# Per-call entries for the weight stream's fill table in the three mixers, and three weight low parts per layer on VectorE

## The chip, the cores and the metric

The kernel runs on one core of one Trainium2 chip. The metric is the device time of one execution, in microseconds. One program computes one inference step of a two-layer network and is written in Bass with the Tile framework: the framework puts every instruction into the queue of its engine, in an order that its scheduler decides at build time, and adds the semaphores.

## The reference, cut to what matters

T = 640 tokens (128 of a prompt, 512 latent) of width D = 1024 pass through two layers. All is float32.

```
h = h + gate_a * MixerBlock(RMSNorm(h) * (1 + scale_a) + shift_a)
h = h + gate_f * SwiGLU(RMSNorm(h) * (1 + scale_f) + shift_f)
MixerBlock: one input projection feeds three branches
  A  multi-head latent attention (8 heads, softmax per block of 128 queries)
  B  bidirectional gated linear attention (GLA; 4 heads, chunks of 64, a state from chunk to chunk)
  C  bidirectional gated DeltaNet (short convolution on q/k/v, decay per head, chunks of 64, a state)
  each branch -> 1024 by its own projection, merged by per-channel sigmoid gates, one output projection
```

## The kernel before, in words

**Products.** Activations lie with channels on the 128 partitions and tokens along the row, as tiles of 128x640. A product with a weight is made of three products of rounded parts: high weight by high activation, high by low, low by high (`mm_k`, L469 to L475). Each is two matmuls of 128x320, so one 128-row step of the contraction is six matmuls on L474. `gm` is their PSUM tile, `xh`/`xl` the parts of the layer's input, `oh`/`ol` those of a branch's output, `ah`/`al` those of the feed-forward.

**The stream.** Nearly all weight products of a layer stand in one list of fixed order, class `Stream` (L284), object `G`: the input projection column by column, then the gates, the branch projections and so on. One *piece* is one such step of six matmuls (`step`), entered in the books at 0.82 us. Weights come for four steps at a time: `wload` (L452) puts a DMA of 256 KB in the queue of SP, and `wsplit` (L460) makes the high part `wh` on ACT (L465, a Copy that rounds) and the low part `wl` on POOL (L466, a subtraction); three such splits may be alive. When the last step of a product has been issued, its `post` runs, which takes the result out of PSUM.

**The fill sites.** The mixers (DeltaNet, attention, GLA, and the state chains, "ch", which belong to the DeltaNet) have chains of small operations across PE, ACT, DVE and POOL. Between these the code calls `fill(name)` (L1502), which looks up a number of microseconds in the table `FILL` (L217) under "site@layer" and lets `G` emit pieces until that debt is paid, as long as the next product's post is registered. A site inside a loop has one number for all its calls. At a few places `G.to(name)` forces everything up to a named product and clears the debt. So the table decides how many pieces of a fixed list stand in which gap, and what an early site takes is missing later: at `G.to` before the merge of the branches the list always stands at the same place. The Tile scheduler then moves instructions by priorities of its own (a split is put ahead by 50), so a piece stands near its site, not at it.

**Sites and lines that matter here.** `l2b`, `prekk`, `vtok`, `kk_products1` belong to the DeltaNet's preparation; `advance1`, `advance2`, `queries1` to attention (L1052 ff.: scores `psc` L1141/L1147, exponential and scaling `pp` on ACT L1152/L1154, turning `ppt` L1162, values `pmo` L1179); `s01` to `s44` to GLA (`gla`, L1258 ff.: chunk products `gpa` L1343, `pu` L1370, then the state chain on DVE, L1378, a run of 14 dependent operations that writes `S`, then the output `gpo` L1395 and L1398, its norm on ACT and DVE L1400 to L1407, and the turn `gpt` L1417); `steps` to the DeltaNet's state chain (matmuls `ch` L922, DVE L947, L959, L973, ACT L962). The four GLA heads are interleaved by head; the attention's blocks are advanced by a scheduler of calls of which the last have no other stage beside them. `decays` (L786) prepares the DeltaNet's decay factors with two 128x640 tiles per pair of heads: DVE L792, POOL L793, ACT L794, POOL L796; its products with the keys are `pk`, L804.

Of the kernel before, what the change touches and what calls it, by code (L numbers as in the profile page):

```python
# [13 lines left out]
ALU = mybir.AluOpType  # L14
AX = mybir.AxisListType
PSUM = bass.MemoryType.PSUM
DRAM = bass.MemoryType.DRAM
# [121 lines left out]
def _layout(inp):  # L139
# [130 lines left out]
}  # L270
OPT = {
    'lat': 'dk0', 'dec': 1, 'l2': 1, 'tick': 3, 'gla0': 1, 'ng2': 7, 'st': 10, 'mc': 20, 'msite': [3], 'ng0':
# [11 lines left out]
class Stream:  # L284
    """Matrix products in a fixed order, emitted piece by piece between other work."""

# [86 lines left out]
def tile_hybrid(ctx: ExitStack, tc, a):  # L373
    nc = tc.nc
    ve, se, ge, pe = nc.vector, nc.scalar, nc.gpsimd, nc.tensor
# [71 lines left out]
    def prio(name):  # L447
# [4 lines left out]
        tc.cur_priority = p + tc.cur_priority - q  # L452

    def wload(src):
        with prio("pl"):
            wr = wp.tile([P, 512], F32, name="wr", tag="wr")
            dma(wr[:, :src.shape[-1]], src)
            return wr

    def wsplit(wr, kt):  # L460
        w = kt * P
        with prio("pw"):
            wh = wp.tile([P, 512], F32R, name="wh", tag="wh")
            wl = wp.tile([P, 512], F32R, name="wl", tag="wl")
            se.activation(wh[:, :w], wr[:, :w], AF.Copy)  # L465
            ge.tensor_tensor(wl[:, :w], wr[:, :w], wh[:, :w], op=ALU.subtract)  # L466
            return wh, wl
# [32 lines left out]

    # ---- modulation
    def mod_load(f, pool_):
# [19 lines left out]
    class ModVe:  # L522
        """Products of the condition with rows of the modulation weights, in single steps of the vector engine."""

# [57 lines left out]

    # ---- residual, norms
    HS = (slice(0, HF), slice(HF, T))
# [70 lines left out]
    def join(name, hs, nm, after, pre=None):  # L655
        """The last residual tile, the norm and its use, by halves of the tokens."""
        if pre:
# [9 lines left out]

    # ---- DRAM scratch
    NB = [dp.tile([4, 2, NCH, 64, 64], F32, name=f"NB{d}") for d in range(2)]
# [6 lines left out]

    # ---- gated DeltaNet
    def gdn_gates(prm, misc, gp, X, fill):
# [108 lines left out]
    def decays(p, E, SC, SCn, gp):  # L787
        N_ = []
        for d in range(2):
# [3 lines left out]
            ge.tensor_tensor(x, x, cst("negf" if d == 0 else "negb").unsqueeze(1).to_broadcast([P, NCH, 64]), op=ALU.add)  # L793
            se.activation(x, x, AF.Exp)  # L794
            N_.append(gp.tile([P, NCH, 64], F32, name="nn", tag="nn", bufs=4))
            ge.tensor_tensor(N_[d], x, SCn[:, :, i].unsqueeze(2).to_broadcast([P, NCH, 64]), op=ALU.mult)  # L796
# [23 lines left out]
    def turn_pairs(src, dst, scale):  # L820
        """Both heads of a pair from channels to tokens, chunk by chunk."""
        pv = psg("pvt").rearrange("p a (j c) -> p (a j) c", c=P)
# [12 lines left out]
    def gdn_solve(lp):  # L835
        Bb = lp.tile([P, 10, P], F32, name="Bb")
        ge.memset(Bb, 0.0)
        for d in range(2):
# [26 lines left out]
            for f in range(2):  # L865
# [11 lines left out]
                def narrow(w):  # L877
                    """Bb[:, g].T @ w[:, g] for all g, by the narrow operand and a turn."""
                    pw = psb([P, 3, P], "pw")
# [148 lines left out]

    # ---- latent attention
    def latents(l, prm, misc, M, pj, gg, fill):  # L1030
# [223 lines left out]

    # ---- gated linear attention
    def gla(l, prm, misc, gp, oh, ol, gmf, gmb, fill, tick):
# [182 lines left out]

    # ---- the order of the large products  # L1440
    pieces = []
# [7 lines left out]
    for l in range(L):  # L1449
# [39 lines left out]
        for gi, (f0, f1) in enumerate(GROUPS):  # L1489
# [3 lines left out]
            for d in range(8):  # L1493
                job(f"fo{gi}_{d}.{l}", a["wfo"][l, d, :, f0 * P:f1 * P], f1 - f0, ("a",),
                    "post" if (gi, d) == (1, 7) else None)
    cur = {}

# [3 lines left out]
    G = Stream(pieces, wload, wsplit, lambda: psg("gm"), mm_any, 3)  # L1501
    G.prio = prio  # L1502
    def fill(name):
        G.fill(FILL[f"{name}@{cur['l']}"])

# [31 lines left out]

    # ---- the layers
    hctx = pool("hp0", "right")
# [304 lines left out]
```

## Time and profile before

| | |
|---|---|
| Runs, us | 2890.33, 2895.8, 2896.3 (median 2895.8) |
| Profiled execution: span from first to last instruction | 2896.0 us |
| Profiled execution: own time beside that span | the page gives the span alone; it lies between the median and the slowest run |
| TensorE (PE) busy | 2721.4 us, 94%, 19444 matmuls |
| DVE, ACT, POOL busy | 53%, 42%, 41% |
| Mean granted TensorE clock | 0.968 |

The mixers take 40 to 876 us (layer 0) and 1476 to 2306 us (layer 1) of the span: first the DeltaNet's preparation (40 to 255, 1476 to 1680), then attention (to 484, to 1903), GLA (to 628, to 2078) and the state chains (to 876, to 2306). The merge and the feed-forward follow. PE is the engine to watch: a microsecond in which it waits, or in which its granted clock is at half, is a microsecond of the span. A wait stands in brackets behind an instruction in the timeline, and in the last column of a group of instructions, each with the instruction that ended it.

### The profile page before, as it was taken

The numbers are of one execution on the slowest core, as the hardware profiler recorded it, in microseconds if no ns is written. First come the engines' busy times: TensorE is split into PE (matmuls) and PEld (weight loads), VectorE is DVE, ScalarE is ACT, GpSimd is POOL, SyncE is SP. The second block draws the span as 40 slices with busy tenths as digits, with TensorE's granted clock in tenths as the row PEclk, the third lists the DMA queues.
The fourth block names the chain that finished last, engine by engine and source line by source line (L and its number), as shares of the span: only waits on it lengthen the run. The fifth ranks groups of instructions, "written<-read, shape, count | busy, mean of one in ns | idle before, by whom it ended". The sixth has DMA issues, their size and how long they took to land. (4 is left out here: it accounts for less than half of the span.)

```text
span 2896.0 us, 49763 instructions
## 1 busy us (share of the span) xinstructions
PE 2721.4 (94%) x19444; PEld 2498.5 (86%) x19444; DVE 1542.6 (53%) x2834; ACT 1209.0 (42%) x2276; POOL 1196.0 (41%) x872
## 2 busy tenths in 40 slices
PE   7899999889999999999998899987999999999998
PEld 4788888778779899999988888876877898999998
DVE  4765584747655699177358576556334334211212
ACT  5575655543333522122366645554333344222223
POOL 3543222333325467366445323233333264443443
PEclk9999999999999999999999999998999999999999
DMA  6254433245433355344323534332423231222222
GB/s 207 90 161 141 91 82 94 88 130 168 140 101 127 108 189 177 86 139 156 105 84 110 177 90 97 72 93 73 137 79 88 73 111 59 77 73 78 73 74 83
DMA packets 291834, 317.10 MB, mean 109 GB/s; under 512 B 163696, under 2 KB 174768, under 8 KB 291472
## 3 DMA queue, kind: packets, MB, share of 16 engines
q1 hardware_dynamic: 291600, 313.92, 37.3%
q8 instruction: 154, 2.52, 0.4%
q14 instruction: 80, 0.66, 0.1%
HBM read 266.01 MB, written 47.82 MB: 108 GB/s over the span
## 5 line engine op out<-in xcount | busy, mean ns | idle before, releaser
L466 POOL TENSOR_TENSOR wl<-wr,wh 128x512 fp32r<-128x512 f32 (+1 forms) x576 | 813.9, 1416 | 1307.0 <-ACT wh L465 1177.0
L474 PE MATMUL gm<-xh,wh 128*128 128x320 f32 x3456 | 846.2, 322 | 25.1 <-ACT xh L624 9.4
L474 PE MATMUL gm<-xh,wl 128*128 128x320 f32 x3456 | 826.8, 316 | 13.4 <-POOL wl L466 13.4
L474 PE MATMUL gm<-xl,wh 128*128 128x320 f32 x3456 | 832.5, 317 | 7.2 <-DVE xl L631 4.2
L465 ACT ACTIVATE wh<-wr 128x512 fp32r<-128x512 f32 (+1 forms) x576 | 357.6, 623 | 944.0 <-PE gm L474 648.9
L474 PEld LDWEIGHTS gm<-xh,wh 128*128 128x128 f32 x3456 | 589.6, 192 | 52.5 <-ACT xh L624 14.5
L474 PEld LDWEIGHTS gm<-xl,wh 128*128 128x128 f32 x3456 | 594.3, 192 | 25.0 <-DVE xl L631 9.8
L474 PEld LDWEIGHTS gm<-xh,wl 128*128 128x128 f32 x3456 | 592.6, 192 | 21.7 <-POOL wl L466 15.5
L549 DVE CUSTOM_DVE_ANT_0 ctb<-wmt,cbb 128x1024 f32<-128x1024 f32 (+1 forms) x200 | 298.6, 1493 | 3.4
L637 DVE SCALAR_TENSOR_TENSOR h<-gm,mod,h 128x128 f32<-128x128 f32 x144 | 55.7, 462 | 272.2 <-PE gm L474 266.1
L474 PE MATMUL gm<-ah,wh 128*128 128x320 f32 x704 | 164.6, 310 | 0.5 <-DVE h L637 0.5
L474 PE MATMUL gm<-ah,wl 128*128 128x320 f32 x704 | 164.1, 309 | 0.0
L474 PE MATMUL gm<-al,wh 128*128 128x320 f32 x704 | 163.9, 309 | 0.0
L962 ACT ACTIVATE VN<-ch 64x64 f32<-64x64 f32 x320 | 70.0, 219 | 178.5 <-DVE vs L959 164.5
L474 PEld LDWEIGHTS gm<-ah,wh 128*128 128x128 f32 x704 | 118.7, 188 | 1.6 <-DVE h L637 1.5
L474 PEld LDWEIGHTS gm<-al,wh 128*128 128x128 f32 x704 | 118.5, 188 | 0.2
L474 PEld LDWEIGHTS gm<-ah,wl 128*128 128x128 f32 x704 | 118.5, 188 | 0.0
L1773 DVE TENSOR_TENSOR th<-th,gm 128x640 f32<-128x640 f32 x44 | 36.2, 822 | 149.2 <-PE gm L474 148.4
L1766 DVE SCALAR_TENSOR_TENSOR th<-th,gm 128x640 f32<-128x640 f32 x44 | 35.9, 816 | 138.3 <-ACT th L1765 138.3
L479 POOL TENSOR_TENSOR al<-th,ah 128x640 fp32r<-128x640 f32 x44 | 89.5, 2033 | 28.0 <-DVE ah L478 28.0
L474 PE MATMUL gm<-ol,wh 128*128 128x320 f32 x384 | 99.3, 332 | 1.5 <-POOL ol L479 1.5
L474 PE MATMUL gm<-oh,wh 128*128 128x320 f32 x384 | 98.7, 334 | 0.5 <-DVE gth L1524 0.3
(747 smaller groups left out, 3822.8 us busy)
## 6 DMA issues: line engine op xcount, KB each, us to landing
wr<-in_wall_dram SPq DMA_DIRECT2D x432, 256.0 KB, 3.0
wmt<-in_wmodt_dram SPq DMA_DIRECT2D x60, 512.0 KB, 3.7
wr<-in_wfo_dram SPq DMA_DIRECT2D x64, 256.0 KB, 2.6
wr<-in_wbr_dram SPq DMA_DIRECT2D x48, 256.0 KB, 2.7
wmt<-in_wmodt_dram SPq DMA_DIRECT2D x40, 256.0 KB, 3.2
wm<-in_wmod_dram SPq DMA_DIRECT2D x16, 512.0 KB, 8.3
wr<-in_wfo_dram SPq DMA_DIRECT2D x32, 192.0 KB, 2.4
h<-in_xt_dram SPq DMA_DIRECT2D x16, 320.0 KB, 5.5
```

What stands on the lines that cost most here:

```text
L465: se.activation(wh[:, :w], wr[:, :w], AF.Copy)
L466: ge.tensor_tensor(wl[:, :w], wr[:, :w], wh[:, :w], op=ALU.subtract)
L474: pe.matmul(ps[:, c, :HF], w_[:, wsl], x_[kx][:, c * HF:(c + 1) * HF], start=(start and i == 0), stop=(stop and i == 2))
L479: (lo or ge).tensor_tensor(dst_l, src, dst_h, op=ALU.subtract)
L549: ins = ve.tensor_tensor_reduce(self.t, wm, self.c[:, i], 0.5, 0.0, ALU.mult, ALU.add, accum_out=acc[h][:, m - m0, i:i + 1])
L637: ve.scalar_tensor_tensor(hs[d][:, s:e], ps[:, c, s - c * HF:e - c * HF], g[:, d, i:i + 1], hs[d][:, s:e], op0=ALU.mult, op1=ALU.add)
L962: se.activation(VN[d * 64:(d + 1) * 64, h, n], ps[h * 64:(h + 1) * 64, 1], AF.Copy)
L1766: ve.scalar_tensor_tensor(v3(th), v3(th), 1.0, ps, op0=ALU.add, op1=ALU.mult)
L1773: ve.tensor_tensor(v3(th), v3(th), ps, op=ALU.mult)
```

## The change

There are two parts. First, `fill` counts the calls of each site in each layer, and adds to the site's number an entry of a new table, `MORE`, which is keyed by site, layer and call: 29 entries in layer 0 with a sum of 41.70 us, 28 in layer 1 with 53.09 us, 94.8 us of the stream's books in all, which is some 116 pieces (694 matmuls, the weights of 29 loads). Second, in `decays`, at the first pair of heads and the first direction of each layer, a counter is set to 3, and the next three splits put their low part on DVE instead of POOL. Apart from that, some comments and docstrings are gone. Lines after the table move down by 16 to 21: L474 is now L493, L466 L485, L792 L811, L761 L780, L766 L785, L1395 L1416, L1398 L1419, L1417 L1438.

```
+MORE = {
+    'l2b0@0#0': 2.13, 'kk_products1_0@0#1': 3.25, 'kk_products1_1@0#1': 0.69, 'kk_products1_2@0#1': 2.39,
...
+    'advance2@0#39': 0.85, 's21@0#0': 4.11, 's24@0#1': 1.77, 's43_0@0#0': 1.93, 's21@0#1': 1.05,
...
+    'advance2@1#19': 5.16, 'advance1@1#25': 1.16, 'advance2@1#24': 0.62, 's01@1#0': 0.63, 's21@1#0': 3.66,
...
+    'steps1_0@1#0': 0.87, 'steps2_0@1#0': 1., 'steps4_0@1#0': 1.2, 'steps4_1@1#0': 1.22, 'steps4_3@1#0':
+    0.99
+}
...
+    cur = {}
...
             se.activation(wh[:, :w], wr[:, :w], AF.Copy)
-            ge.tensor_tensor(wl[:, :w], wr[:, :w], wh[:, :w], op=ALU.subtract)
+            cur["lows"] = cur.get("lows", 0) - 1
+            (ve if cur["lows"] >= 0 else ge).tensor_tensor(wl[:, :w], wr[:, :w], wh[:, :w], op=ALU.subtract)
...
             se.activation(x, x, AF.Exp)
+            if p == 0 and d == 0:
+                cur["lows"] = 3
             N_.append(gp.tile([P, NCH, 64], F32, name="nn", tag="nn", bufs=4))
...
+    calls = {}
...
     def fill(name):
-        G.fill(FILL[f"{name}@{cur['l']}"])
+        key = f"{name}@{cur['l']}"
+        n = calls[key] = calls.get(key, -1) + 1
+        G.fill(FILL[key] + MORE.get(f"{key}#{n}", 0.0))
```

**DVE, layer 0, the first call of `decays`** (some 120 us into the span). `ex` are the decay tiles, `kq` and `kbd` the normalised queries and keys, `cy` the convolution's sums, `wl` a weight's low part. Before:

```order
L723 COPY SC<-scp 128x320
L724 TENSOR_SCALAR SCn<-SC 128x80
L792 TENSOR_TENSOR ex<-ex,SC 128x640 x4
L761 SCALAR_TENSOR_TENSOR kq_518<-cy,crs 128x640 x2
L766 COPY kbd_519<-kq_518 64x10x64 x2
L744 SCALAR_TENSOR_TENSOR cy<-cx,prm_162,cy 128x127
L744 SCALAR_TENSOR_TENSOR cy<-cx,prm_162,cy 128x511
```

and now:

```order
L742 COPY SC<-scp 128x320
L743 TENSOR_SCALAR SCn<-SC 128x80
L811 TENSOR_TENSOR ex<-ex,SC 128x640 x2
L485 TENSOR_TENSOR wl<-wr,wh 128x512
L811 TENSOR_TENSOR ex<-ex,SC 128x640 x2
L780 SCALAR_TENSOR_TENSOR kq_518<-cy,crs 128x640
L485 TENSOR_TENSOR wl<-wr,wh 128x512
L785 COPY kbd_519<-kq_518 64x10x64 x2
L763 SCALAR_TENSOR_TENSOR cy<-cx,prm_162,cy 128x127
L763 SCALAR_TENSOR_TENSOR cy<-cx,prm_162,cy 128x511
L764 SCALAR_TENSOR_TENSOR cy<-cx,prm_162,cy 128x127
L764 SCALAR_TENSOR_TENSOR cy<-cx,prm_162,cy 128x511
```

The two low parts shown stand in this row now, and the third follows two operations after the last row; the two `kq` of a pair, neighbours before, stand apart. POOL has these three fewer.

**PE, layer 1, GLA, output of the first head.** Before:

```order
L474 MATMUL gm<-xh,wl 128x320 x2
L1395 MATMUL gpo<-gvt,asum 128x128
L1398 MATMUL gpo<-S,gq 64x128 x2
L1395 MATMUL gpo<-gvt,asum 128x128 x2
L474 MATMUL gm<-xh,wh 128x320 x2
L474 MATMUL gm<-xl,wh 128x320 x2
L474 MATMUL gm<-xh,wl 128x320 x2
L1398 MATMUL gpo<-S,gq 64x128
L474 MATMUL gm<-oh,wh 128x320 x2
L1398 MATMUL gpo<-S,gq 64x128
```

and now:

```order
L493 MATMUL gm<-xl,wh 128x320 x2
L493 MATMUL gm<-xh,wl 128x320 x2
L493 MATMUL gm<-xh,wh 128x320 x2
L493 MATMUL gm<-xl,wh 128x320 x2
L493 MATMUL gm<-xh,wl 128x320 x2
L1416 MATMUL gpo<-gvt,asum 128x128
L1419 MATMUL gpo<-S,gq 64x128 x2
L1416 MATMUL gpo<-gvt,asum 128x128
L1419 MATMUL gpo<-S,gq 64x128 x2
L1416 MATMUL gpo<-gvt,asum 128x128
L1419 MATMUL gpo<-S,gq 64x128 x2
```

Before, one piece stood between the products `pu` of this head and its first output product, and single stream matmuls stood among the output products. Now 51 stream matmuls stand between `pu` and the first `gpo`, and none among the five groups of output products.

**PE, layer 1, GLA, output and turn of the last head.** Before, the end of the output products:

```order
L1395 MATMUL gpo<-gvt,asum 128x128
L1398 MATMUL gpo<-S,gq 64x128 x2
L1395 MATMUL gpo<-gvt,asum 128x128
L1398 MATMUL gpo<-S,gq 64x128 x2
L474 MATMUL gm<-xh,wh 128x320 x2
L474 MATMUL gm<-xl,wh 128x320 x2
L474 MATMUL gm<-xh,wl 128x320 x2
```

with 102 stream matmuls from there to the turn `gpt` on L1417; and now:

```order
L1416 MATMUL gpo<-gvt,asum 128x128
L1419 MATMUL gpo<-S,gq 64x128 x2
L1416 MATMUL gpo<-gvt,asum 128x128
L1419 MATMUL gpo<-S,gq 64x128 x2
L1416 MATMUL gpo<-gvt,asum 128x128
L1419 MATMUL gpo<-S,gq 64x128 x2
L1438 MATMUL gpt<-C_base,go 128x128 x5
L493 MATMUL gm<-oh,wh 128x320 x2
L493 MATMUL gm<-xh,wh 128x320 x2
```

No stream matmul stands between the last output product and the turn of its result. In layer 0 the same two places have 42 stream matmuls between them before, and 6 now. From the merge of the branches on, the order on PE is the same in both kernels.

## Rows read from the trace of the kernel before

**Rows 1.** The page's line of PE, and the core's span and mean granted clock.

```profile
PE 2721.4 (94%) x19444; PEld 2498.5 (86%) x19444; DVE 1542.6 (53%) x2834; ACT 1209.0 (42%) x2276; POOL 1196.0 (41%) x872
...
core 0: 2896.0 us, clock 0.968
```

**Rows 2.** Windows: us; busy (x count) of PE, PEld, DVE, ACT, POOL; PEclk, DMA share, GB/s.

```profile
40.00:876.00 836.00, 776.91 (x5845) 676.78 (x5843) 520.72 (x1122) 421.49 (x837) 295.03 (x224) 0.97 0.42 114
1476.00:2306.00 830.00, 765.37 (x5790) 671.86 (x5790) 462.66 (x936) 409.96 (x812) 286.07 (x218) 0.96 0.36 100
...
1050.00:1100.00 50.00, 50.00 (x343) 50.00 (x342) 49.15 (x55) 11.23 (x18) 33.76 (x18) 1.00 0.59 185
```

**Rows 3.** Groups on PE, 40 to 2306 us: busy, mean ns | idle before, by releaser.

```profile
L474 PE MATMUL gm<-xh,wl 128*128 128x320 f32 x2603 | 627.8, 318 | 13.4 <-POOL wl L466 13.4
...
L1162 PE MATMUL ppt<-C_base,pp 128*128 128x128 f32 x336 | 52.2, 279 | 7.8 <-ACT pp L1154 7.2 <-DVE pT L1167 0.4 <-DVE st L1151 0.2
...
L1398 PE MATMUL gpo<-S,gq 128*64 128x128 f32 x160 | 26.4, 380 | 16.1 <-DVE S L1378 16.1
...
L804 PE MATMUL pk<-kq,kbd 128*128 128x128 f32 x160 | 23.9, 292 | 12.7 <-DVE nn L808 11.6 <-DVE kbd L766 1.0
...
L1370 PE MATMUL pu<-gvt,ez 128*128 128x128 f32 x160 | 21.4, 281 | 6.3 <-ACT us L1372 5.5 <-ACT ez L1355 0.8
...
L1343 PE MATMUL gpa<-gq,kz 128*64 128x64 f32 x320 | 12.5, 236 | 12.8 <-DVE th L1419 5.0 <-POOL gt L1335 3.9 <-DVE kz L1334 3.5
...
L1141 PE MATMUL psc<-kbh,qh 128*128 128x128 f32 x16 | 4.4, 272 | 5.9 <-ACT pp L1152 5.0 <-ACT pj L1225 0.9
```

**Rows 4.** Timeline, the first `decays` of layer 0 (123 to 135 us), then layer 1's.

```profile
126.72 0.46 PE L474 MATMUL gm<-xl,wh 128*128 128x320 f32 x2
...
128.15 3.34 POOL L796 TENSOR_TENSOR nn<-ex,SCn 128x640 f32<-128x640 f32 x2
...
131.46 2.79 POOL L466 TENSOR_TENSOR wl<-wr,wh 128x512 fp32r<-128x512 f32 x2
...
133.01 0.90 PE L474 MATMUL gm<-xh,wl 128*128 128x320 f32 x2 [4.51 <-POOL wl L466]
...
133.71 0.73 PE L474 MATMUL gm<-xh,wh 128*128 128x320 f32 x2
```

```profile
1548.86 0.90 PE L474 MATMUL gm<-xh,wl 128*128 128x320 f32 x2 [4.82 <-POOL wl L466]
```

**Rows 5.** Groups on DVE by form, 100 to 150 us.

```profile
L761 DVE SCALAR_TENSOR_TENSOR kq<-cy,crs 128x640 f32<-128x640 f32 x2 | 4.3, 2191 | 0.0
L747 DVE SCALAR_TENSOR_TENSOR cy<-cx,cy 128x640 f32<-128x640 f32 x5 | 4.1, 823 | 2.7 <-ACT cx L746 2.6
```

**Rows 6.** Groups on ACT by form, 40 to 255 us.

```profile
L465 ACT ACTIVATE wh<-wr 128x512 fp32r<-128x512 f32 x41 | 25.1, 622 | 19.4 <-issue 10.9 <-PE gm L474 8.4
L742 ACT ACTIVATE cy<-gm,prm 128x640 f32<-128x640 f32 x12 | 9.4, 787 | 1.0 <-DVE kq L761 1.0
```

**Rows 7.** Timeline, layer 1, end of the last GLA head.

```profile
2041.99 0.70 PE L1398 MATMUL gpo<-S,gq 128*64 128x128 f32 x4
...
2047.99 1.28 ACT L488 ACT_TABLE_LOAD   x1
...
2049.53 0.82 DVE L1407 TENSOR_TENSOR go<-go,grs 128x640 f32<-128x640 f32 x1 [4.58 <-ACT grs L488]
```

**Rows 8.** Window at the end of layer 0's attention, where no stream matmul stands.

```profile
470.00:484.00 14.00, 11.78 (x103) 8.84 (x102) 4.86 (x16) 9.81 (x19) 4.99 (x8) 1.00 0.64 165
```

**Rows 9.** Timeline, one step of the state chain near its end, layer 1.

```profile
2282.72 0.45 PE L922 MATMUL ch<-S,bd_k 64*64 64x64 f32 x8
...
2284.87 0.92 ACT L962 ACTIVATE VN<-ch 64x64 f32<-64x64 f32 x4 [0.20 <-DVE vs L959]
...
2286.06 0.50 DVE L973 SCALAR_TENSOR_TENSOR S<-S,GE,ch 128x64 f32<-128x64 f32 x2 [1.03 <-ACT VN L962]
...
2287.19 0.45 PE L922 MATMUL ch<-S,bd_k 64*64 64x64 f32 x8
```

More of the change, by code (lines that the diff above doesn't have):

```diff
@@ L1495, in tile_hybrid @@
                     "post" if (gi, d) == (1, 7) else None)
-    cur = {}
     def mm_any(ps, w, kw, kx, xs, start, stop, half):
```

8 rows, old and new, of the table MORE are left out of this document.

## Prediction, made before the changed kernel was run

> **What bounds the kernel now.** I read the page's busy shares first. PE is busy for 2721.4 us of a span of 2896.0, and its granted clock is 0.968 on average [rows 1]. So PE sets the time, and a change can win only what PE waits, or what it does at the lower of its two clock levels. The windows by stage come next, because an average over stages hides where that is. In the merge and the feed-forward PE is full: in 50 us there it is busy for 50.00 with 343 matmuls, 0.146 us each, so a piece of six takes 0.875 us [rows 2]. In the mixers it is not. It is busy for 776.91 of 836 us in layer 0 and for 765.37 of 830 in layer 1, so it waits 59.1 + 64.6 = **123.7 us**. The clock there is 0.97 and 0.96; read as a share of time at 1.2 GHz instead of 2.4, that is 836 x 0.06 + 830 x 0.08, some 117 us at half clock [rows 2]. Third, PE's groups with the idle time ahead of them say what ends the waits. The output of GLA waits 16.1 us for the state chain on DVE; `gpa` 12.8 and `pu` 6.3 us for other parts of GLA; `pk` 12.7 for the DeltaNet's decays; attention's `ppt` 7.8 and `psc` 5.9 for the exponentials; and the stream itself 13.4 for low parts from POOL [rows 3]. Each is a gap into which pieces of the stream could go, if PE's order had them there.
>
> **The change, part by part.** The median of the three runs is 2895.8 us and the profiled span 2896.0. The sum is made against 2896.0, and the two count as one.
>
> Low parts on DVE. In `decays` the stream's matmul on `wl` waits 4.51 us in layer 0 and 4.82 in layer 1: POOL makes two decay products first (`nn`, 3.34 us) and then the two low parts (2.79) [rows 4]. On DVE they stand in the order shown among the decays, ahead of the keys, so both waits should go: 4.51 + 4.82 = **-9.3**. What it costs on DVE is hidden, as PE does not wait for DVE in this place; it would cost if DVE became late there (fourth rival). The nearest rows for one operation on a full tile are 823 ns and 2191 ns (two forms of the same operation; the second ran while POOL was busy) [rows 5]. Six of them lie between 4.9 and 13.1 us, over two layers.
>
> Pieces into the waits. I laid the changed order on PE beside the old one and counted, for each wait, the stream matmuls that now stand ahead of it. Those of `gpo` on `S` are covered entirely: 16.1 of 16.1; ahead of the first head's in layer 1 there are 51 stream matmuls now, 7.4 us. Of `pk` it is 11.9 of 12.7; of `gpa` 5.1 of 12.8; of attention 17.0, out of `ppt`, `psc` and smaller groups of that stage; of `pu` 1.7 of 6.3 [rows 3]; five smaller groups give 7.7. Together 59.5 us. I do not take all of it. A piece brings work to the very engine that ends many of these waits: a quarter of a `wh` copy of 622 ns on ACT, and a share of an eviction of 787 ns per product [rows 6], some 0.3 us for each 0.875 us of PE. So I take three quarters, **-44.6**. The ends are -59.5 (the pieces' own ACT work is hidden) and -30 (half of it is given back). The loads that come earlier use DMA that is busy for 0.36 to 0.42 of these windows [rows 2]; SP only issues them, and they are costed at nothing, because the loads run ahead of the splits. If they were late, the stream itself would wait (third rival).
>
> What is missing later. The stream's length to the merge is fixed, so each piece moved forward is taken from something behind. Three places lose cover.
>
> The ends of GLA: the last output product ends at 2041.99 + 0.70 = 2042.69, and its normalised result is there at 2049.53 + 0.82 = 2050.35 [rows 7]. That is a chain of ACT and DVE of 7.7 us, two table loads of 1.28 among it, with 102 stream matmuls in between before and none now in layer 1, and 42 before and 6 now in layer 0. PE waits 7.7 in layer 1 and 7.7 - 0.9 = 6.8 in layer 0: **+14.5**. At the least, with both tables loaded while ACT waits, it is 2 x (7.7 - 2 x 1.28) = 10.2; the upper end is 2 x 7.7.
>
> The ends of attention: with the stream at its end, PE waits 14 - 11.78 = 2.2 of 14 us in layer 0 [rows 8], which is 0.19 us for each us of work. The order takes 72 and 120 stream matmuls (10.5 and 17.5 us) out of stretches of 31 and 49 us, so 52 us of attention's own work are left bare: 52 x 0.19 = **+9.8**. The ends are 0 and the whole of the cover, 28.
>
> The ends of the state chains: a covered step takes 2287.19 - 2282.72 = 4.47 us with 18 stream matmuls, 2.63 us, in it [rows 9]. Of a bare step I take 0.8 us as idle: half of `VN`'s 0.92 us, half of `S`'s 0.50 and the handing over, because the first halves release the next matmuls. The order takes 60 matmuls from steps with 18 in layer 1 and 68 from steps with 13.6 in layer 0, 8.3 steps: **+6.7** (ends 0 and 8.3 x 2.63 = 22).
>
> The clock. Behind the wait of 4.51 us a pair of matmuls shows 0.90 and 0.73 us, against 0.46 ahead of it [rows 4]: half clock. If the 117 us of half clock follow the waits in proportion, the 9.3 + 59.5 us of waits that go hold 65 us of it. What is lost of a microsecond at half clock lies between 0.37 (0.46 for 0.73) and a half; at 0.45 that is 29 us at most. As the new waits bring their own, I take a third: **-10** (ends 0 and -29).
>
> The Trainium skill ("TensorE: Matmul & The Clock Gate", "Why this matters for your kernels") advises keeping TensorE free of idle gaps between bursts, since its throughput drops behind them. The row of 0.73 us agrees for this wait; by that rule alone the clock's term would be -29 and the sum 19 us lower.
>
> Sum: 2896.0 - 9.3 - 44.6 + 14.5 + 9.8 + 6.7 - 10 = **2863**.
>
> **The rivals.**
>
> *The pieces are only moved (slower).* Were the stretches behind to keep their length, since their own chains and not PE set them, they would lose all their cover: attention 192 x 0.146 = 28, chains 128 x 0.146 = 18.7, GLA's ends 138 x 0.146 = 20.1, together 66.8, against 9.3 + 44.6 gained. 2896 + 13 = **2909**. It decides from the point where the stretches keep over four fifths (53.9 / 66.8) of the cover they lose. Against it: the bare window of attention waits only 16% [rows 8]. For it: the mixers' waits are chains of latency throughout [rows 3].
>
> *The clock stays up.* All 59.5 us go and the clock's whole share with them: -9.3 - 59.5 + 31 - 29 = -66.8, **2829**. For it: the pair of 0.73 us [rows 4]; against it: the new waits at the three ends.
>
> *The pieces wait for their own weights (the pieces stand in place but do not cover).* The splits come through ACT and POOL, busy already in these stages, and three may be alive. If half of what the pieces cover is given back so: 2863 + 22 = **2885**. For it: the stream waits 13.4 us for low parts already [rows 3]. Against: in those 13.4, 9.3 belong to the two places that the change frees.
>
> *DVE becomes late at the decays.* If the low parts push the keys out there: six times the difference of the two rows, 6 x (2.19 - 0.82) = 8.2 [rows 5], and two more pairs of norms split between table loads, 4 x 1.28 = 5.1 [rows 7]. So +13.3 less what the gaps there still hide, some 12: **2875**. The Trainium skill ("GPSIMD Engine Reference", "1. Specifications") says that GpSimd shares its SBUF interfaces with VectorE and that they contend when a DVE instruction has two SBUF inputs. The 2191 ns beside a busy POOL against 823 agrees with it.
>
> **How the numbers follow.** Forecast 2863: chance 0.55; moved only 0.08; clock 0.10; waiting for weights 0.17; DVE late 0.10. The range: downward 14.9 (all 59.5), 9.5 (half of the rest of the clock) and 4.3 (ends of GLA at 10.2) make 2863 - 29 = 2834; upward the third rival's 2885 with the low parts' gain lost as well (9.3) makes 2893 after rounding down. That leaves out the first two rivals, 0.18. A measurement of this kernel can tell 0.2%, 5.8 us, from no change; faster by that is below 2890. Faster: all of the forecast, the clock and the DVE case, and most of the third rival, 0.85. Slower: the first rival and a little of the third, 0.09. Same: 0.06.
>
> **What would show it.** Right: `gpo` on `S` waits under 2 us in place of 16.1, `pk` under 3, the stream on `wl` about 4 in place of 13.4; new rows of `gpt` on the normalised `go`, about 7 us in each layer; PE's wait in the mixers falls from 123.7 to about 101; and `wl` on DVE ahead of the keys at the first decays. The clock's term is right if the mixers' granted clock rises from 0.97 and 0.96 by about one hundredth. Wrong: if the attention's end waits over 20 us more, the first rival holds; if the stream's rows show waits for `wh` or `wl` over 20 us, the third; if `pk` still waits for `kbd` or `nn` for 10 us, the fourth. The merge and the feed-forward should not change.

## The result and the profile after

The changed kernel takes 2966.06 us (median of 4 runs, 2964.54 to 2967.07), the kernel before 2896.05 us (median of 4). The ratio is 1.0241, with a 95% interval of 1.0228 to 1.0255: **70 us slower**, where 33 us faster was forecast and 2893 was the upper end of the range.

The page and the core of the changed kernel, against [rows 1]:

```profile
span 2964.2 us, 49778 instructions
...
PE 2752.6 (93%) x19444; PEld 2525.7 (85%) x19444; DVE 1535.8 (52%) x2840; ACT 1207.7 (41%) x2278; POOL 1174.0 (40%) x866
...
core 0: 2964.2 us, clock 0.948
```

The number of matmuls is the same. PE is busy for 31 us more (2752.6 for 2721.4), and waits 37 us more (211.6 for 174.6). As the matmuls are the same, the longer busy time can be read as the clock's share. The clock went the wrong way: read as time at half clock, 0.052 x 2 x 2964 = 308 us after and 0.032 x 2 x 2896 = 185 before. The two windows that answer to the mixers [rows 2], and then the merge of layer 0:

```profile
40.00:925.00 885.00, 800.24 (x5862) 698.06 (x5863) 518.54 (x1126) 426.17 (x841) 285.76 (x222) 0.92 0.39 107
1525.00:2375.00 850.00, 775.61 (x5818) 680.50 (x5818) 454.95 (x939) 404.64 (x810) 274.76 (x214) 0.94 0.36 97
925.00:1018.00 93.00, 89.83 (x627) 87.95 (x623) 57.41 (x86) 38.30 (x62) 55.33 (x35) 0.99 0.48 154
```

Layer 0's mixers are 49 us longer (885 for 836), layer 1's 20 (850 for 830), and the rest is as before. PE waits 84.8 and 74.4 us there, 159 in place of 123.7. The groups on PE that answer to [rows 3], and five that were small before:

```profile
L493 PE MATMUL gm<-xh,wl 128*128 128x320 f32 x2603 | 626.9, 318 | 9.7 <-DVE wl L485 5.1 <-POOL wl L485 4.6
...
L1183 PE MATMUL ppt<-C_base,pp 128*128 128x128 f32 x336 | 55.2, 290 | 13.2 <-ACT pp L1175 10.2 <-DVE pj L1254 2.7 <-DVE pT L1188 0.3
...
L943 PE MATMUL ch<-vs,bd_kt 64*64 64x64 f32 x576 | 49.6, 256 | 9.1 <-ACT VN L983 6.3 <-DVE vs L980 1.1
...
L1168 PE MATMUL psc<-kbh,qh 128*128 128x320 f32 x128 | 37.0, 370 | 11.5 <-ACT pp L1173 10.7 <-DVE pT L1188 0.2 <-ACT pj L1246 0.2
...
L513 PE MATMUL cs<-cx,bones 128*128 128x320 f32 x64 | 26.0, 546 | 18.0 <-ACT crs L505 8.5 <-ACT kt L848 5.5 <-ACT cy L761 4.0
L1416 PE MATMUL gpo<-gvt,asum 128*128 128x128 f32 x80 | 24.5, 398 | 9.1 <-ACT gvt L1332 9.1
L1419 PE MATMUL gpo<-S,gq 128*64 128x128 f32 x160 | 22.8, 375 | 3.6 <-DVE S L1399 3.6
L825 PE MATMUL pk<-kq,kbd 128*128 128x128 f32 x160 | 22.4, 280 | 1.3 <-DVE nn L829 1.3
L1391 PE MATMUL pu<-gvt,ez 128*128 128x128 f32 x160 | 20.4, 279 | 0.0
...
L1364 PE MATMUL gpa<-gq,kz 128*64 128x64 f32 x320 | 13.9, 248 | 11.6 <-POOL gt L1356 8.7 <-DVE th L1440 1.7 <-DVE kz L1355 1.1
...
L1438 PE MATMUL gpt<-C_base,go 128*128 128x128 f32 x40 | 7.2, 321 | 14.4 <-DVE go L1428 14.4
```

So three of the waits at which the pieces were aimed are gone: `gpo` on `S` 3.6 us in place of 16.1, `pk` 1.3 for 12.7, `pu` 0.0 for 6.3. That is 30 us. `gpa` keeps 11.6 of 12.8. Others took their place: `gpt` on `go` 14.4 for 2.4, `gpo` on `gvt` 9.1 for 3.2, `cs` 18.0 where it had 3.3, `ch` 9.1 for 3.3, the scores `psc` of the large form 11.5 for 3.4, `ppt` 13.2 for 7.8.

To see where the time is, I took instructions that both programs have (the k-th matmul of a name) as marks, and compared when they start. Between two marks, "net" is the difference in length less 0.146 us [rows 2] for each stream matmul that the stretch has more, or plus 0.146 for each that it has fewer. A net of zero means that pieces came or went at their full price and nothing else happened.

| stretch (start in the kernel before, us) | stream matmuls, change | length, us | net, us | PE waits, before, after | half clock, before, after |
|---|---|---|---|---|---|
| layer 0: to the first `gpa` (500) | +5 | +15.8 | **+15.0** | 46.6, 59.3 | 37.5, 53.5 |
| GLA, to its last outputs (612) | +121 | +15.4 | -2.2 | 13.9, 10.7 | 19.3, 21.6 |
| to the first chain step (644) | -34 | +6.2 | **+11.2** | 0.9, 8.4 | 4.6, 20.5 |
| chains and merge (970) | -92 | +10.4 | **+23.9** | 6.7, 15.2 | 6.8, 58.0 |
| layer 1: 1449 to the first `gpa` (1920) | +7 | +11.4 | **+10.4** | 43.1, 51.4 | 37.5, 50.0 |
| GLA, to its last outputs (2040) | +173 | +10.3 | **-15.0** | 21.2, 12.8 | 34.1, 21.7 |
| to the first chain step (2080) | -88 | -4.1 | **+8.8** | 0.7, 8.3 | 6.8, 17.1 |
| chains and merge (2398) | -92 | +1.6 | **+15.0** | 5.2, 9.2 | 6.8, 27.3 |

With 1.3 in layer 0's feed-forward the nets make about 68, the difference of the two spans (2964.2 - 2896.0 = 68.2). Only GLA gains. (Stretches that an edit does not touch differ by up to 3 us between the profiled executions below, so a net of that size says nothing.)

### The profile page after: what moved, and what is told of

Same layout as the page of the kernel before. It is cut to its first block, busy times and chain, and to the rows that moved or that the text cites. A ratio compares the mean times of both kernels' runs of the same rounds, so it can differ in the third digit from the quotient of the medians.

```text
span 2964.2 us, 49778 instructions
## 1 busy us (share of the span) xinstructions
PE 2752.6 (93%) x19444; PEld 2525.7 (85%) x19444; DVE 1535.8 (52%) x2840; ACT 1207.7 (41%) x2278; POOL 1174.0 (40%) x866
## 5 line engine op out<-in xcount | busy, mean ns | idle before, releaser
L485 POOL TENSOR_TENSOR wl<-wr,wh 128x512 fp32r<-128x512 f32 (+1 forms) x570 | 797.8, 1402 | 1293.5 <-ACT wh L483 1150.6
L493 PE MATMUL gm<-xh,wh 128*128 128x320 f32 x3456 | 842.4, 322 | 29.0 <-ACT xh L643 9.7
L493 PE MATMUL gm<-xl,wh 128*128 128x320 f32 x3456 | 832.0, 318 | 8.7 <-DVE xl L650 5.0
L493 PE MATMUL gm<-xh,wl 128*128 128x320 f32 x3456 | 826.5, 317 | 9.7 <-DVE wl L485 5.1
L493 PEld LDWEIGHTS gm<-xh,wh 128*128 128x128 f32 x3456 | 591.9, 193 | 53.7 <-ACT xh L643 14.8
L493 PEld LDWEIGHTS gm<-xl,wh 128*128 128x128 f32 x3456 | 596.6, 193 | 24.6 <-DVE xl L650 10.6
L493 PEld LDWEIGHTS gm<-xh,wl 128*128 128x128 f32 x3456 | 595.6, 193 | 16.9 <-POOL wl L485 5.9
L493 PE MATMUL gm<-ah,wh 128*128 128x320 f32 x704 | 164.6, 310 | 0.5 <-DVE h L656 0.5
L493 PE MATMUL gm<-ah,wl 128*128 128x320 f32 x704 | 164.0, 309 | 0.0
L493 PE MATMUL gm<-al,wh 128*128 128x320 f32 x704 | 164.0, 309 | 0.0
L493 PEld LDWEIGHTS gm<-ah,wh 128*128 128x128 f32 x704 | 118.6, 188 | 1.6 <-DVE h L656 1.5
L493 PEld LDWEIGHTS gm<-al,wh 128*128 128x128 f32 x704 | 118.5, 188 | 0.2
L493 PEld LDWEIGHTS gm<-ah,wl 128*128 128x128 f32 x704 | 118.6, 188 | 0.0
L493 PE MATMUL gm<-oh,wh 128*128 128x320 f32 x384 | 100.9, 340 | 7.0 <-DVE oh L497 5.1
L493 PE MATMUL gm<-ol,wh 128*128 128x320 f32 x384 | 100.5, 335 | 4.4 <-POOL ol L498 4.4
```

Source lines behind the costliest of these rows:

```text
L485: (ve if cur["lows"] >= 0 else ge).tensor_tensor(wl[:, :w], wr[:, :w], wh[:, :w], op=ALU.subtract)
L493: pe.matmul(ps[:, c, :HF], w_[:, wsl], x_[kx][:, c * HF:(c + 1) * HF], start=(start and i == 0), stop=(stop and i == 2))
```

## The experiments

**The two parts of the change, and two groups of its entries.** First run: the table `MORE` empty. Second: `cur["lows"] = 0`, so that the low parts stay on POOL. Third and fourth: as the second, with a part of the table.

```
lows alone:        MORE = {}
table alone:       cur["lows"] = 0
GLA's entries:     cur["lows"] = 0; MORE = entries of the sites s01 to s44
preparation:       cur["lows"] = 0; MORE = entries of l2b, prekk, vtok, kk_products1, advance, queries1
```

> The kernel before with the second part of the change alone: three low parts per layer on DVE, the new table empty. Theory A (the low parts are a small gain, the pieces do the harm): the two waits of the stream on POOL (4.51 and 4.82 us) go and 5 to 9 us are won, 2887 to 2891 us. Rival B (the low parts push the DeltaNet's norms and keys out, and that is what makes the change slow): 2905 us or more, with waits of pk or of cs of several us at the first decays.

> The change without its second part: the whole new table, all low parts on POOL. Theory A: the pieces do the harm, so 2966 to 2978 us, the changed kernel plus what the low parts win. Rival B: 2863 to 2900 us, since without the low parts on DVE the pieces fill their waits.

> The kernel before plus the table's entries of GLA's sites alone (18.47 us in layer 0, 26.40 in layer 1). Theory A (what is taken from the bare ends is paid there, the more so at half clock): the waits of gpo on S go from 16 to under 5 us, but the ends of GLA and the last steps of the state chains give it back and more, 2895 to 2920 us. Rival C (GLA's entries are sound, and the DeltaNet's and the attention's do the harm): 2875 to 2890 us.

> The kernel before plus the table's entries of the DeltaNet's preparation and of attention alone (19.0 us in layer 0, 21.4 in layer 1). Theory A: the waits inside move to other instructions of the same chains (cs, psc, ppt), and the ends of attention and what lies behind lose their cover, 2915 to 2940 us. Rival D (these stages are only pushed back by the pieces' own time, which the end gives back): 2890 to 2900 us.

Measured: the low parts alone 2890.5 us (ratio 0.9984, 0.9973 to 0.9995); the table alone 2972.54 (1.0258, 1.023 to 1.0286); GLA's entries 2940.71 (1.0152, 1.0132 to 1.0172); the preparation's and attention's 2924.81 (1.01, 1.0082 to 1.0118); the kernel before, measured beside them, 2895.36. So the pieces do the harm, +77 us, and the low parts win 5. Rival B falls, and so do rivals C and D: each group of entries loses by itself. My sizes were too small: GLA's entries cost 45 us where I had allowed 25.

The low parts win 5 us, but not as forecast. The stream's group on PE, 40 to 2306 us, with the low parts alone (the same statement as L474; the line numbers of the runs shift with their tables):

```profile
L479 PE MATMUL gm<-xh,wl 128*128 128x320 f32 x2600 | 627.3, 318 | 12.4 <-DVE wl L471 9.9 <-POOL wl L471 2.5
```

At the same two places it waits for DVE now, 3.99 and 5.87 us, where it waited 4.51 and 4.82 for POOL. What is won in the waits comes behind: `pk` waits 10.3 us in place of 12.7. The rest of the 5 us isn't told from the scatter between executions.

In the run with GLA's entries the stretches of the table above read: GLA -5.3 and -13.9 us net, the ends of GLA +10.8 and +9.0, layer 0's chains and merge **+38.4**, layer 1's +5.8. GLA gains 19 us, about what was forecast, and the stretches behind lose 64. Groups on PE of that run, 40 to 2355 us; the first has 3.2 us before, the last is the turn of GLA's outputs:

```profile
L1402 PE MATMUL gpo<-gvt,asum 128*128 128x128 f32 x80 | 24.0, 390 | 9.1 <-ACT gvt L1318 9.1
L1405 PE MATMUL gpo<-S,gq 128*64 128x128 f32 x160 | 21.9, 362 | 3.6 <-DVE S L1385 3.6
...
L1424 PE MATMUL gpt<-C_base,go 128*128 128x128 f32 x40 | 7.2, 320 | 14.5 <-DVE go L1414 14.5
```

**The state chains, with their cover given back.** To the run with GLA's entries I added, where the stream has no piece left at a site of the chains, matmuls that nobody reads:

```
         G.fill(FILL[key] + MORE.get(f"{key}#{n}", 0.0))
+        if name.startswith(("steps", "ch")) and not G.ready():
+            cur["junk"] = cur.get("junk", 0.0) + FILL[key]
+            if cur["junk"] > 0:
+                ps = psg("gm")
+                while cur["junk"] > 0:
+                    cur["junk"] -= 0.82
+                    for i in range(3):
+                        for c in range(2):
+                            pe.matmul(ps[:, c, :HF], xh[:, i, 0:P], xh[:, i + 1, c * HF:(c + 1) * HF],
+                                      start=i == 0, stop=i == 2)
```

> The run with GLA's entries alone (2941 us), plus 264 matmuls whose result nobody reads: from the point where the stream has no piece left in the state chains, each site of a chain emits such matmuls at the rate of its number in the old table. Theory A1 (the bare steps are long because the clock falls to half there): the half-clock time of 61 us in the last third of layer 0's chains falls under 20, and the kernel gets faster although PE has 264 matmuls (38 us at full clock) more to do: 2915 to 2932 us. Rival (the bare steps are as long as their chain of ACT and DVE, whatever the clock): the added matmuls vanish in idle time, 2936 to 2946 us. Rival (PE's own work sets these steps): 2955 us or more.

Measured: 2961.31 us (1.0239, 1.0215 to 1.0263), 20.6 us above the run without them. Theory A1's time is missed: of the added 38.5 us (264 x 0.146) only 18 come back, and the time lies in the range of the last rival (2955 us or more). The half-clock time that should fall from 61 to under 20 us falls to 27. The steps themselves show what each is right about. The table has the last pair of heads of layer 0's chains. A step is counted as in [rows 9], from one group of eight `ch` on `S` to the next; each entry is its time and the stream's, or unread, matmuls in it, beside its 24 matmuls `ch` and at most ten `pqs`; h marks a step mostly at half clock.

| kernel | six steps, us / matmuls |
|---|---|
| before | 4.5/12, 4.4/11, 4.4/11, 4.4/11, 4.7/6, 3.9/9 |
| changed | 2.7/0, 3.0/0 h, 3.1/0 h, **6.5/6 h**, **7.1/9 h**, 5.0/3 h |
| GLA's entries | 3.3/0, 3.0/0 h, 3.1/0 h, **6.5/6 h**, **7.1/9 h**, 5.0/3 h |
| the same with unread matmuls | 4.5/14, 4.4/11, 4.4/11, 4.4/11, 4.4/11, 4.4/11 |

And windows with most of these steps: with GLA's entries alone (the whole, then 4 us ahead of the fall of the clock, then 12 us behind it), and last the whole with the unread matmuls:

```profile
884.00:910.00 26.00, 23.32 (x164) 15.23 (x165) 10.99 (x41) 6.18 (x25) 1.49 (x1) 0.62 0.04 12
886.00:890.00 4.00, 2.16 (x34) 1.35 (x32) 3.16 (x14) 1.53 (x5) 1.49 (x1) 1.00 0.18 66
898.00:910.00 12.00, 12.00 (x62) 7.89 (x63) 2.82 (x10) 1.43 (x7) 0.00 (x0) 0.50 0.01 1
```

```profile
884.00:910.00 26.00, 26.00 (x213) 17.56 (x212) 11.20 (x44) 6.28 (x25) 1.66 (x1) 1.00 0.05 12
```

A bare step is short, 3.0 us, even at half clock, and PE waits little in it. Eleven unread matmuls lengthen it to 4.4 us, most of their price of 1.6: that is the last rival's part. But the clock falls while the steps are bare, and when the stream goes on it goes on at half clock: 7.1 us for a step with nine stream matmuls and two `pqs`, where 4.4 us are enough for eleven at full clock. That is A1's part. With the unread matmuls the six steps have 51 matmuls more and take 26.2 us in place of 27.9; to the end of this pair of heads it is 96 more, worth 14.0 us, for 3.8 us of time. By the marks, layer 0's chains and merge fall from +38.4 us net to +23.9 with the unread matmuls counted at their price. The rest stays: the half clock in the earlier pairs of heads, where the stream has pieces and no unread matmul is added.

The fall isn't given by the program alone. At the end of layer 1's chains the changed kernel and the table alone have the same steps in the same order, a bare one and then three with 6, 9 and 3 stream matmuls, and PE is busy for 2.11 of 3.00 us in the bare one in both. In the profiled execution of the changed kernel (the first two lines) the clock fell behind it, in that of the table alone it didn't:

```profile
2347.00:2350.00 3.00, 2.11 (x32) 1.54 (x30) 1.27 (x6) 1.90 (x6) 1.27 (x1) 1.00 0.14 29
2351.00:2368.00 17.00, 16.39 (x86) 10.68 (x85) 4.33 (x16) 2.62 (x12) 0.00 (x0) 0.50 0.00 0
```

```profile
2351.00:2354.00 3.00, 2.11 (x29) 1.53 (x28) 1.23 (x5) 2.13 (x6) 1.27 (x1) 1.00 0.03 9
2355.00:2366.00 11.00, 10.47 (x94) 7.03 (x93) 4.43 (x16) 2.61 (x12) 0.00 (x0) 1.00 0.00 1
```

The three steps behind it took 6.45, 7.07 and 4.96 us at half clock, and 4.09, 4.30 and 3.39 at full. So this difference, 6.7 us for 18 us at half clock, is the clock's alone. It is also most of why layer 1's chains and merge, with 92 stream matmuls less in both, cost +15.0 us net in the changed kernel and +6.4 in the table alone. What decides between a fall and none isn't shown.

**The chains' own entries, and attention's first ones.**

```
chains:      cur["lows"] = 0; MORE = entries of the sites steps1 to steps4
attention:   cur["lows"] = 0; MORE = 'advance1@0#0', 'advance1@0#1', 'advance2@0#0', 'advance1@0#3', 'queries1@0#5'
```

> The kernel before plus the table's entries of the state chains alone (4.20 us in layer 0, 5.28 in layer 1), at the chains' first steps. Theory A (parts add up): 77 - 45 - 29 leaves 0 to 5 us, 2895 to 2901 us. Rival (the last steps lose their cover and fall to half clock by this alone): 2905 us or more.

> The kernel before plus five entries of the first calls of layer 0's attention alone (6.36 us, some 8 pieces). Theory A (pieces in front of the first scores delay the pipeline of ACT and DVE that later waits hang on, so the stage grows by the pieces' own time, and its end loses cover as well): 2900 to 2910 us, with the first stretch of attention 5 to 7 us longer than the pieces' own time. Rival D (the pieces are neutral here, and the loss of the whole table came from the DeltaNet's entries): 2893 to 2898 us.

Measured: the chains' entries 2896.26 us (1.0012, 1.0 to 1.0024), against 2894.96 for the kernel before, so no loss that is clear of the noise; their pieces stay within the chains. The parts add up: 45.4 + 29.4 + 1.3 - 4.9 = 71 us, and the change costs 70. Attention's five entries: 2900.22 (1.0023, 1.0013 to 1.0032), 5 us slower, as theory A said, but by another split than it said: the first stretch grows by 2 to 3 us net and not by 5 to 7, a stretch in the middle (385 to 395 us before) by some 4, and the end of attention, where the pieces are missing, by some 7, of which a part comes back behind. The waits of `psc` and `ppt` that they were aimed at (5.9, 3.4 and 7.8 us before) did not shrink in sum; the groups on PE, 40 to 2306 us:

```profile
L1169 PE MATMUL ppt<-C_base,pp 128*128 128x128 f32 x336 | 54.5, 287 | 10.5 <-ACT pp L1161 6.0 <-DVE pj L1240 3.6 <-DVE st L862 0.7
L1154 PE MATMUL psc<-kbh,qh 128*128 128x320 f32 x128 | 35.3, 358 | 4.5 <-ACT pp L1159 3.8 <-DVE pj L1240 0.5
L1148 PE MATMUL psc<-kbh,qh 128*128 128x128 f32 x16 | 4.4, 272 | 6.1 <-ACT pp L1159 5.0 <-ACT pj L1232 1.1
```

**The DeltaNet's entries, and one of them.**

```
DeltaNet:    cur["lows"] = 0; MORE = entries of l2b, prekk, vtok, kk_products1
one entry:   cur["lows"] = 0; MORE = {'l2b0@0#0': 2.13}
```

> The kernel before plus the table's entries of the DeltaNet's preparation alone (9.62 us in layer 0, 8.60 in layer 1). Theory A2 (these pieces fill pk's waits of 12.7 us, but they split pairs of norms on ACT, and the end of the preparation and of attention pays): 2898 to 2908 us, with 4 waits or fewer of over 2 us on crs in place of those on nn. Rival F (the DeltaNet's entries gain, and attention alone makes the loss of 29 us): 2882 to 2893 us.

> The kernel before plus a single entry of the table, 2.13 us (three pieces) at the first norms of layer 0's DeltaNet; the pieces stand between the two column sums of one pair of norms. In its order on ACT the exponentials of the decays now come ahead of the first of the two norms, and the two norms stand apart. Theory A2 (it is the order that the pieces bring on ACT, not their own time): a wait of 8 to 11 us of the second column sum on the first norm, as in the changed kernel, and a loss of 2 to 8 us at the end of the DeltaNet's preparation in layer 0, 2897 to 2904 us. Rival (the wait is only where the pieces' time is spent, and the stage does not get longer): 2893 to 2897 us.

Measured: the DeltaNet's entries 2907.18 us (1.0049, 1.003 to 1.0067), 11.5 us slower, as theory A2 said; if the parts add up here too, attention's have the other 18 of 29 (they were not run by themselves). The waits moved from `pk` (12.7 before) to `cs` (3.3 before), in the groups on PE, 40 to 2320 us:

```profile
L499 PE MATMUL cs<-cx,bones 128*128 128x320 f32 x64 | 24.9, 527 | 19.6 <-ACT crs L491 10.4 <-ACT cy L747 5.4 <-ACT kt L834 3.8
...
L811 PE MATMUL pk<-kq,kbd 128*128 128x128 f32 x160 | 23.1, 285 | 3.1 <-DVE nn L815 3.1
```

One entry of three pieces brings the largest of them by itself. The kernel with `l2b0@0#0` alone takes 2898.64 us (1.0018, 1.0005 to 1.0031; the kernel before, measured beside it, 2892.39). Its timeline at the first `decays` (start, us, engine, line, what, and in brackets the wait and what ended it):

```profile
122.28 0.74 ACT L799 ACTIVATE ex<-ex 128x640 f32<-128x640 f32 x1 [2.73 <-POOL ex L798]
...
126.16 0.74 ACT L799 ACTIVATE ex<-ex 128x640 f32<-128x640 f32 x1 [3.14 <-POOL ex L798]
126.91 1.28 ACT L491 ACT_TABLE_LOAD   x1
...
128.21 0.79 ACT L491 ACTIVATE crs<-cs,epsD 128x640 f32<-128x640 f32 x1
...
129.05 2.50 PE L499 MATMUL cs<-cx,bones 128*128 128x320 f32 x4 [10.44 <-ACT crs L491]
```

With the pieces ahead of them the column sums come later. So on ACT two exponentials, which wait for POOL, now stand ahead of the norm `crs`, and the next column sum waits 10.44 us for the norm to have read the last one. The time loses less than that wait, 1.4 to 9 us by the interval: before, `pk` waited 3.09 us and the stream 4.51 in this place, and both waits are gone. By the marks the way to the first `gpa` is only 2.1 us net longer, so where the 6 us are isn't told from the scatter.

**Pieces in a wait, paid from a surplus.** If the gain is real and the source is what costs, nine pieces in the three waits on `S` of GLA's layer 1 should gain when they come from a filler with pieces to spare. The last site of GLA in layer 1 emits 102 stream matmuls, 14.9 us, over a chain of 7.7 us [rows 7].

```
-    's44_3@1': 14.68
+    's44_3@1': 7.4
+MORE = {'s21@1#0': 2.46, 's21@1#1': 2.46, 's21@1#2': 2.46}
```

By the books that is nine pieces at the three sites; by the marks 48 stream matmuls, eight pieces, move. Three kernels: this with the low parts on DVE; the same without the cut of the filler, so that the state chains pay; the first without the low parts.

> The kernel before with the three low parts on DVE, three pieces each at the first call of the site ahead of the state chain of GLA's first three heads in layer 1, and the number of the last GLA site of that layer cut from 14.68 to 7.4 us, so that the nine pieces come from a filler that is longer than the 7.7 us it covers, and the chains keep theirs. Theory A (a piece in a wait gains, what costs is the cover taken from bare ends): the three waits of 3.2, 3.2 and 3.4 us on S fall under 1 us each and the kernel is faster than with the low parts alone, 2880 to 2886 us. Rival E (pieces ahead of a wait delay the chain behind it by as much as they fill): 2888 to 2894 us.

> As the run with nine pieces in GLA's layer 1 (2874 us), but the number of the last GLA site stays at 14.68 us: the same pieces in the same waits, now taken from the state chains of layer 1 in place of the long filler at GLA's end. Theory A2 (the source decides: cover taken from a surplus is free, cover taken from the chains is paid): 2878 to 2886 us, 4 to 12 us above the run before, and the loss stands in the last steps of layer 1's chains. Rival (nine pieces are too few for the chains to feel): 2872 to 2877 us.

> The run with nine pieces in GLA's layer 1 and the shortened filler, but all low parts on POOL as before. Theory A2 (pieces and low parts add up): 2876 to 2882 us, the gain of the nine pieces alone, 14 to 18 us. Rival (most of the 21 us came from the low parts together with a better start): 2884 to 2892 us.

Measured: **2874.02 us** (0.9927, 0.991 to 0.9945), 21 us faster than the kernel before and the fastest of all; paid by the chains 2886.32 (0.9972, 0.9961 to 0.9983); without the low parts 2880.51 (0.9952, 0.9939 to 0.9966). The first is faster than theory A's range, the second a little slower than A2's (0.3 us), the third lies in its range. Same pieces, same waits: 12 us lie between the two sources. By the marks, GLA in layer 1 gains 16 us in each of the three, and in the second the stretch from GLA's last output to the end of the merge loses 10, where the first loses nothing. Only half of the 10 stands in the chains and the merge (4.9), where A2 had expected all. The other half stands ahead of the chains: there the stream, eight pieces further than before, comes to a product whose operand `ol`, the low part of a branch's output, isn't ready, and a stretch at half clock follows:

```profile
2054.79 0.90 PE L479 MATMUL gm<-ol,wh 128*128 128x320 f32 x2 [2.44 <-POOL ol L484]
```

The group of `gpo` on `S` in layer 1's GLA, in the kernel before (1885 to 2090 us) and in the first of the three (1885 to 2080):

```profile
L1398 PE MATMUL gpo<-S,gq 128*64 128x128 f32 x80 | 14.4, 397 | 11.7 <-DVE S L1378 11.7
```

```profile
L1405 PE MATMUL gpo<-S,gq 128*64 128x128 f32 x80 | 10.8, 339 | 5.0 <-DVE S L1385 5.0
```

The first and the last head still wait for `S`, 1.9 and 2.7 us, so "under 1 us each" holds for the second and third head alone. Between the first `gpa` of the second head and that of the last, nine pieces remove 7.0 us of waiting (14.4 to 7.4) and with it all of the 20.4 us at half clock. The gain there is 16.3 us, so what is left for the clock is 9.3 us, 0.46 for each microsecond at half clock.

## Why the prediction was wrong, step by step

Two steps failed. The chains were priced by the idle time of a bare step, without what the clock does behind it: +38.9 us in place of +5.7. And waits in the preparation and attention were counted as filled, each by itself, where the pieces only moved them: with the low parts a loss of 11.8 us in place of a gain of 34.1. Term by term, with the net of the marks:

| term | forecast | measured |
|---|---|---|
| low parts, and pieces in the preparation and attention | -9.3 - 24.8 = -34.1 | +11.8 |
| the ends of attention | +9.8 | +13.6 |
| pieces in GLA | -18.9 | -17.2 |
| the ends of GLA | +14.5 | +20.0 |
| the chains and the merge, pieces and bare steps | -1.0 + 6.7 = +5.7 | +38.9 |
| clock | -10 | within the rows above |

(24.8, 18.9 and 1.0 are three quarters of 33.0, 25.2 and 1.3 us of waits counted as covered; the recorded text doesn't say how its five smaller groups, 7.7 us, are shared out, so this split is made here. The ends of attention are 442 to 483 and 1855 to 1903 us before; they lose 72 and 117 stream matmuls.)

**Low parts: sign right, size half, reason wrong.** -4.9 in place of -9.3. The step that failed is "both waits should go": alone, the low parts only change the engine that is waited for, 9.9 us on DVE for 9.3 on POOL. A part of the fourth rival's mechanism is there: in the changed kernel's timeline at the first `decays` the low part on DVE lasts 2.02 us beside a busy POOL, where POOL took 1.4 [rows 4]; the third one, with POOL idle, takes 0.68. With the low parts alone, the ones that the stream waits for take 1.65, over 1.1 us of it beside POOL. The rival's price, 12 us, and its sign, 10 us of `pk` on `nn` or `kbd`, are not there.

```profile
120.40 2.02 DVE L485 TENSOR_TENSOR wl<-wr,wh 128x512 fp32r<-128x512 f32 x1
...
139.11 0.68 DVE L485 TENSOR_TENSOR wl<-wr,wh 128x512 fp32r<-128x512 f32 x1
```

**Pieces into the waits: wrong in the preparation and attention, right in GLA by luck of the size.** The step that failed is the counting itself: "for each wait, the stream matmuls that now stand ahead of it", each wait taken by itself. In the preparation and attention the waits are links of chains on ACT, DVE and POOL whose order the pieces change as well; I read the new order on PE and DVE and took the waits on ACT from the old trace. The run with one entry shows that by three pieces (`cs` 10.44 us on `crs`). In attention pieces ahead of the first scores left the waits on `pp` as they were. What each of attention's other entries does was not tried. In GLA -17.2 stands for -18.9, but not by the waits alone: of 25.2 us that were to be filled, 11.6 went (35.1 to 23.5 in the table of stretches), as `gpa` kept its waits and `gpo` on `gvt` got new ones. The rest came with 10 us less at half clock, which the forecast had in another term.

**The ends of GLA: right in kind, the sum by luck.** The forecast row of `gpt` on `go` is there with 14.4 us against 14.5. But the two ends have only 5.16 and 5.30 of it, 10.5 us, near the forecast's lower end of 10.2; the rest stands at the turns of other heads (2.4 in all before). The chain of 7.7 us [rows 7] was read where stream work stood in it: ACT waited 1.64 us for the stream's matmuls and made a `wh` of 0.63 between the chain's own operations. Bare, it takes 5.1 us. Net the ends cost 20.0, as the waits there grow by 15.1 and the time at half clock by 26 us. The timeline of the one in layer 1, which answers to [rows 7], and the turn in layer 0:

```profile
2112.47 0.70 PE L1419 MATMUL gpo<-S,gq 128*64 128x128 f32 x4
...
2114.30 1.28 ACT L505 ACT_TABLE_LOAD   x1
...
2117.45 0.82 DVE L1428 TENSOR_TENSOR go<-go,grs 128x640 f32<-128x640 f32 x1 [2.31 <-ACT grs L507]
2118.33 1.33 PE L1438 MATMUL gpt<-C_base,go 128*128 128x128 f32 x5 [5.16 <-DVE go L1428]
```

```profile
653.46 1.33 PE L1438 MATMUL gpt<-C_base,go 128*128 128x128 f32 x5 [5.30 <-DVE go L1428]
```

**The chains: the price was off by a factor of nearly seven.** "0.8 us as idle" for a bare step is about right for the wait alone: three bare steps of the changed kernel wait 1.04, 0.53 and 0.40 us. What the forecast left out is what a bare step can do to the clock, and so to the steps behind it: 1.6 to 2.8 us for each step of layer 1 that followed at half clock. I had put the clock in one term, with a gain, and its new losses at the ends only in a phrase. The count was short as well: the chains and merges give up 184 stream matmuls (twice 92), where the forecast had 128 in the last steps. A microsecond at half clock isn't a whole one of the span: by the page some 120 us more of it go with 31 us more of PE's busy time, a quarter each, while the steps of layer 1 gave 0.37 and the GLA stretch 0.46.

**The rivals.** The first, "only moved", with a chance of 0.08, is nearest in sign and size, but not in its reason. The bare steps of the chains don't keep their length, and attention's ends wait 4.5 and 6.2 us more, together not the 20 that it named as its sign. Its price, 2909, was too low by 57 us: it too booked 34.1 us of gain in the preparation and attention, which is 46 us off, and it had the chains' cover at full clock, 21 us off; for attention's ends it had 14 too much. The second rival, the clock, points the right way for the three waits of the nine-piece kernel, where 0.46 us for each microsecond at half clock came back. The third doesn't show: the stream waits 9.7 us for `wl` and 3.6 for `wh`, not 20. (The range's upper end is 2885 + 9.3 = 2894, not 2893; nothing hangs on it.) The Trainium skill's rule on idle gaps ("TensorE: Matmul & The Clock Gate", "Why this matters for your kernels") speaks of gaps; in the run with GLA's entries the clock fell at 890 us behind 4 us in which PE was busy for 2.16 and no wait was longer than 1.13 us, so here it took no long gap to lose the clock.

## What to carry to other kernels

A list of fillers of fixed length is a budget: before adding one at a wait, find the place that will go without it, and move pieces only out of covers that are longer than the chain they cover. Price the lost cover by what the clock may do behind it, not by the filler's own time, and read the length of a bare chain where no filler's work stands in it. And where a scheduler orders the engines, read the new order on every engine that ends the wait.

## What was unexpected of the hardware

A stretch of small matmuls on a dependent chain lost the clock with no wait over 1.13 us in it, and then kept half clock through 12 us in which PE was busy all the time. With the stretch filled by more matmuls of 128x320 the clock was 1.00, and the six steps together took less time. And the same steps in the same order, with the same bare step ahead, fell to half clock in one profiled execution and not in another: the one with nine stream matmuls took 7.07 and 4.30 us.

The subtraction of a low part (128x512) took DVE 0.68 us with POOL idle and 2.02 us with POOL busy throughout; POOL itself took 1.4 us for one.
